# Small constants loaded at the end of the up-projections, half of a merge operand written in place, other operand loads cut into pieces

## The chip, the cores and the metric

The kernel runs on the 8 cores of one Trainium2 chip, in two dies of four cores (0 to 3 and 4 to 7). Each core computes one element of a batch of 8, with the same program and no traffic between cores. The metric is the device time of the slowest core, in microseconds (us).

Some executions fall into a slower state.

There is a smaller disturbance too: a few cores have some 160 us at a granted clock of 0.81, and such runs may still count as fast. (Core 0 of the kernel before has 0.81 in its trace's clock record from 75.0 to 236.2 us, with 6.8 us at 0.50 in between, which is 0.80 on average.)

- The **undisturbed cores** of a kernel: of all cores of all its runs, those whose mean clock lies within 0.0055 of the 90th percentile of that kernel's cores. I give the mean of their spans with its standard error.
- The **gain by stage**. The two kernels give TensorE the same instructions in the same order, and both profiles hold all 14317 weight loads. So the time of load number k in one profile, minus its time in the other, is what has been gained up to there, core by core.

## The reference, cut to what matters

```python
h = rms_norm(x, norm[l])
proj = h @ w_in[l]
# A: mLSTM: a short causal convolution (conv_w, conv_b) on q and k, gate biases, head norm (mh_norm)
qk = silu(causal_depthwise_conv(m_qk, conv_w[l], conv_b[l]))
ig = m_i + b_igate[l];  lf = log_sigmoid(m_f + b_fgate[l])
hm = rms_norm(mlstm_chunkwise(mq, mk, mv, ig, lf), mh_norm[l]) * sigmoid(m_o) * silu(m_z)
# B: latent attention
ha = causal_block_attention(qa, ka, v_a) * silu(a_z)
# C: cross attention into 256 memory tokens
hc = memory_attention(c_q, mkv[:, :, 0], mkv[:, :, 1]) * silu(c_z)
# gated merge and output projection
merged = g_m * (hm @ w_br_m[l]) + g_a * (ha @ w_br_a[l]) + g_c * (hc @ w_br_c[l])
x = x + merged @ w_out[l]
return rms_norm(x, final_norm)
```

With 2048 tokens and a width of 2048, `hm`, `ha` and `hc` are 2048 x 1024 each. They reach the merge through DRAM, as HMT, HAT and HCT, and are loaded half by half (1024 tokens, 2 MB).

## The kernel before

The program is written out in full by Python. Two generators are interleaved: a "dense" one (all projections, the merge, the output) and a "side" one (latent attention, then mLSTM, then cross attention). Each `yield` is a point where the other may put its instructions. `fw.op` and `fw.dma` derive the waits from what an instruction reads and writes; a DMA is issued by SyncE ("sp"), ScalarE ("act") or GpSimd ("pool"). A block's weights are 2 MB, loaded by GpSimd in four pieces when the block two before it is done:

```python
def w_done(name):
    wst["free"].append(wloaded.pop(name).slot)
    w_load()                 # 2 MB for the block after next starts here
```

The small constants are loaded at the head of the block that uses them, just after such a `w_done`:

```python
def qk_block(h):
    if h == 0:
        P["cw"] = mem.alloc("cw", [128, 16, 4], F32)
        P["cb"] = mem.alloc("cb", [128, 16], F32)
        fw.dma("sp", P["cw"][:], convw_d, writes=[P["cw"].r])
        fw.dma("sp", P["cb"][:], convb_d, writes=[P["cb"].r])
        # ...
                    act(y[:], bk[:, 0:512], AF.Identity, [r_bk, cw.r, cb.r], [y.r],
                        scale=cw[:, j, 3:4], bias=cb[:, j:j + 1])

def v_block(jv):
    if jv == 0:
        P["bif"] = mem.alloc("bif", [128, 8], F32)
        fw.dma("sp", P["bif"][:], bif_d, writes=[P["bif"].r])
    # ...

def oz_block(h):
    gmh = mem.alloc("gmh", [128, 256], F32)
    fw.dma("sp", gmh[:], gmh_d[:, h * 256:(h + 1) * 256], writes=[gmh.r])
    # ...
```

Cross attention: `loads` fetches queries of 256 KB (CQT), three buffers deep. `turn` transposes 128 tokens of the result and stores them through a ring of two buffers:

```python
def turn(t):
    # ... 8 transposes into btb
    o = hos.next()                       # a ring of 2
    copy("act", o[:], btb, [r_bt], [o.r])
    fw.dma("sp", HCT_d[t // 8, :, t % 8, :], o[:].rearrange("p a b -> p (a b)"), reads=[o.r], ...)
# ... per step of the loop:
    while turns:
        t = turns.pop(0)
        turn(t)
        if t == 7:
            marks.add("HC0")
        yield 0.6
```

The merge loads its operands while cross attention still runs:

```python
def hload(th, b):
    nm, src = (("HMT", HMT_d), ("HAT", HAT_d), ("HCT", HCT_d))[b]
    dims = "p a b c -> p (a b c)" if b != 1 else "p a b -> p (a b)"
    fw.dma("act", hb[b][:].rearrange(dims), src[th].rearrange("p a b -> p (a b)"), ...)   # 2 MB

def hm_ready():
    if "HM1" in marks and not hb:
        # ... allocate hb[0], hb[1], hb[2]
        hload(0, 0)
        hload(0, 1)
# ...
for u in range(LA):                      # LA = 4
    hm_ready()
    if u == LA - 2:
        yield ("need", "HM1")
        hm_ready()
        yield ("need", "HC0")
        hload(0, 2)
    yield from gate_unit(u, sring)       # 32 matmuls, a yield after every 8
```

The softmax here doesn't subtract the row's maximum and nothing guards it: scores larger than these inputs give would overflow.

## Time and profile before

| | before |
|---|---|
| time, median of 4 runs | 2923.26 us (2916.87 to 3257.57) |
| fast runs | 2920.87, 2925.64, 2916.87 us |
| profiled execution, slowest core | 2931.1 us (core 0) |
| TensorE busy on core 0 | 2753.6 us, 94% |
| five waits that the change aims at, core 0 | 10.66 + 9.88 + 4.99 + 16.29 + 3.11 = 44.9 us |

TensorE is the bottleneck (94% of the span busy, and 86% of the chain that ended last), so time can only be won where it idles or runs at a lowered clock. The last line is the DMA queue of ScalarE, with packets, MB and share of 16 engines' time; it carries the operand loads.

Die 0 had a stretch at 0.80 from 75 to 236 us and die 1 had not, as the windows of cores 0 and 4 show. (Columns: start and end in us, length, busy time and instructions of PE, PEld, DVE, ACT and POOL, the granted clock, the DMA share and GB/s.) First core 0:

```profile
75.00:236.00 161.00, 152.87 (x769) 73.82 (x783) 87.03 (x133) 66.17 (x165) 4.24 (x8) 0.80 0.36 98
```

and core 4:

```profile
75.00:236.00 161.00, 141.85 (x835) 69.91 (x832) 101.99 (x162) 67.50 (x168) 4.96 (x9) 0.99 0.38 107
```

In the same 161 us core 0 got through fewer weight loads (783 against 832) although it was busy for longer.

The timeline of TensorE on core 0 at the five waits. Each line is start, duration, engine, line, what it writes from what it reads; in brackets stands the idle time before it and what ended that:

```profile
453.06 0.37 PE L288 MATMUL bk<-Pa_68_3197,vx_52_2581 128*128 128x256 bf16 x1 [10.66 <-ACT Pa_68_3197 L292]
...
621.16 1.88 PE L288 MATMUL bk<-w_11_53,hT_8_50 128*128 128x258 bf16 x8 [9.88 <-DVE GIF_49 L301]
...
789.75 0.26 PE L288 MATMUL bk<-Pa_69_3198,vxb_63_3192 128*128 128x128 bf16 x1 [4.99 <-ACT Pa_69_3198 L292]
...
1685.84 1.01 PE L288 MATMUL bk<-cq_141_17856,kmT_3170 128*128 128x512 bf16 x2 [16.29 <-ACT ho_157_17946 L296]
...
1716.53 1.93 PE L288 MATMUL bk<-cq_142_17857,kmT_3170 128*128 128x512 bf16 x4 [3.11 <-ACT ho_157_17946 L296]
```

A releaser is often only the last link. The chain of waits around the first gap (start, duration, what) shows the rest:

```profile
436.79 14.92 DMA cb_3869<-convb
...
451.80 0.07 ACT y_89_3877 L292
...
452.63 0.29 ACT Pa_68_3197 L292
453.06 1.23 PE bk L288 x3
```

An 8 KB constant took 14.9 us to land. ScalarE stood still until then, and the exponentials that TensorE wanted (`Pa`) were queued behind. ScalarE's own waits (total us, times, longest) name the same constant, and for the fourth and fifth gap the store out of the buffer that `turn` reuses:

```profile
ACT ho_157_17946 L296 <- DMA HCT<-ho_157_17946: 26.4, 3, 17.5
...
ACT y_89_3877 L292 <- DMA cb_3869<-convb: 13.0, 1, 13.0
```

After each of these five waits TensorE ran at half its clock for a while. The trace's clock record of core 0 has 0.50 from 445.8 to 456.0, 616.4 to 626.7, 787.1 to 797.3, 1674.6 to 1691.6 and 1715.5 to 1722.3 us, that is until 2.9 to 7.6 us after the ends of the waits. Windows on core 0, the last one from deep in the merge:

```profile
453.00:456.00 3.00, 2.94 (x8) 1.20 (x9) 2.61 (x6) 1.91 (x5) 0.00 (x0) 0.50 0.00 0
...
1686.00:1692.00 6.00, 5.61 (x17) 1.92 (x16) 0.00 (x0) 2.68 (x5) 0.00 (x0) 0.53 0.52 132
1720.00:2720.00 1000.00, 993.83 (x4564) 454.36 (x4654) 138.91 (x216) 115.98 (x192) 258.82 (x314) 1.00 0.52 89
```

The clock is 0.50 and 0.53 in the two stretches after waits. In the last window TensorE is 99.4% busy at full clock: nothing can be won there.

### The profile page before, as it was taken

The page shows a single profiled execution, that of the slowest core. Times are in us where ns is not written, and L with a number is a line of the kernel's source. Part 1 is how long each engine was busy: PE and PEld are TensorE (multiplying, and loading weights), DVE is VectorE, ACT ScalarE, POOL GpSimd, SP SyncE. Part 2 cuts the span into 40 slices and gives each one's busy share as a digit, 9 for nine tenths or more (in the row PEclk, how much of TensorE's full clock was granted, in tenths as well). Part 3 has the DMA queues.
Part 4 walks back from the last instruction along what each step waited for, and adds up shares of the span by engine and source line. Part 5 has one row for each costly group of instructions (what it writes and reads, how often), then busy time and mean ns, then how long its engine had stood idle before and what let it go on. Part 6 is the DMA issues. An engine that isn't in the chain of part 4 may idle for free.

```text
span 2931.1 us, 42038 instructions; the slowest of 8 cores (2898.1 to 2931.1 us)
## 1 busy us (share of the span) xinstructions
PE 2753.6 (94%) x14042; PEld 1373.2 (47%) x14317; DVE 1104.5 (38%) x2091; ACT 813.5 (28%) x1672; POOL 498.9 (17%) x605
## 2 busy tenths in 40 slices
PE   4998998989999999999889799999999999999998
PEld 2443444566455754444444344444444444444443
DVE  3546537435657447545553331111111111111333
ACT  4523124323435335335444221111111111110111
POOL 0000300000010010124332012222222222222000
PEclk9789999999999999999999999999999999999999
DMA  7603642643443432444543654444455544446562
GB/s 195 188 15 120 179 114 56 136 96 66 108 108 78 109 93 60 97 132 129 138 123 112 176 140 76 78 74 76 79 117 121 104 76 76 77 78 107 189 213 86
DMA packets 143523, 322.16 MB, mean 110 GB/s; under 512 B 14800, under 2 KB 73104, under 8 KB 135120
## 3 DMA queue, kind: packets, MB, share of 16 engines
q0 software_dynamic: 42192, 134.79, 27.8%
q1 hardware_dynamic: 100256, 172.08, 18.6%
q10 hardware_dynamic: 864, 12.58, 1.1%
q8 instruction: 119, 1.95, 0.3%
q14 instruction: 92, 0.75, 0.1%
HBM read 380.38 MB, written 73.79 MB: 155 GB/s over the span
## 4 chain that ended last, share of the span: by engine, by line
PE 86%; DMA 5%; DVE 3%; issue 3%; ACT 2%; SPq 0%; DVEq 0%; POOL 0%; ACTq 0%; POOLq 0%
PE bk L288 85%; DMA xt_14_61<-x 1%; DMA HCT<-ho_158_17947 1%; DMA xt_13_60<-mem 1%; DMA cb_3869<-convb 1%; DMA bif_5641<-bif 0%; DMA xt_13_60<-x 0%; DMA mv_111_13609<-MV 0%; DMA gmh_7714<-g_mh 0%; PE bk L490 0%; DMA QNT<-ob_39_1819 0%; DVE Cf_13628 L308 0%; DMA KRT<-ob_38_1818 0%; DMA HCT<-ho_157_17946 0%; PE bk L516 0%
## 5 line engine op out<-in xcount | busy, mean ns | idle before, releaser
L288 PE MATMUL bk<-w_11_53,hT_8_50 128*128 128x512 bf16 (+1 forms) x1135 | 218.0, 344 | 15.7 <-DVE GIF_49 L301 11.7
L288 PE MATMUL bk<-w_11_53,hT_9_51 128*128 128x512 bf16 (+1 forms) x1132 | 218.5, 341 | 5.7 <-ACT hr_134_13632 L296 2.2
L288 PE MATMUL bk<-hT_8_50,w_10_52 128*128 128x512 bf16 x780 | 184.7, 379 | 5.3 <-ACT hr_134_13632 L296 2.2
L288 PE MATMUL bk<-hT_9_51,w_10_52 128*128 128x512 bf16 x778 | 184.8, 381 | 1.2
L288 PEld LDWEIGHTS bk<-w_11_53,hT_8_50 128*128 128x128 bf16 x1152 | 114.8, 101 | 102.2 <-issue 38.4
L288 PEld LDWEIGHTS bk<-w_11_53,hT_9_51 128*128 128x128 bf16 x1152 | 113.6, 100 | 87.6 <-issue 27.0
L288 PEld LDWEIGHTS bk<-hT_8_50,w_10_52 128*128 128x128 bf16 x800 | 77.3, 98 | 88.5 <-issue 4.9
L288 PEld LDWEIGHTS bk<-hT_9_51,w_10_52 128*128 128x128 bf16 x800 | 78.3, 98 | 84.9 <-issue 1.6
L288 PE MATMUL bk<-hT_8_50,wg_137_17736 128*128 128x512 bf16 x496 | 114.5, 383 | 0.8
L288 PE MATMUL bk<-hT_8_50,wg_138_17737 128*128 128x512 bf16 x498 | 114.4, 383 | 0.7
L308 DVE SCALAR_TENSOR_TENSOR tm_178_19271<-sh_183_19393,bk 128x512 f32<-128x512 f32 x31 | 21.3, 687 | 248.7 <-PE bk L288 248.7
L308 DVE SCALAR_TENSOR_TENSOR tm_178_19271<-sh_185_19395,bk 128x512 f32<-128x512 f32 x31 | 21.3, 687 | 247.5 <-PE bk L288 247.5
L288 PE MATMUL bk<-hT_8_50,wg_139_17738 128*128 128x512 bf16 x497 | 112.7, 379 | 0.8
L288 PE MATMUL bk<-hT_9_51,wg_138_17737 128*128 128x512 bf16 x499 | 112.4, 379 | 0.7
L288 PE MATMUL bk<-hT_9_51,wg_139_17738 128*128 128x512 bf16 x499 | 112.4, 379 | 0.7
L288 PE MATMUL bk<-hT_9_51,wg_137_17736 128*128 128x512 bf16 x496 | 111.8, 379 | 0.8
L292 ACT ACTIVATE sh_183_19393<-bk 128x512 f32<-128x512 f32 x46 | 27.5, 597 | 297.6 <-PE bk L288 297.6
L292 ACT ACTIVATE sh_185_19395<-bk 128x512 f32<-128x512 f32 x46 | 27.5, 597 | 290.2 <-PE bk L288 290.2
L288 PE MATMUL bk<-w_10_52,hT_8_50 128*128 128x512 bf16 x374 | 94.2, 398 | 10.0 <-ACT hT_8_50 L296 9.0
L288 PE MATMUL bk<-w_10_52,hT_9_51 128*128 128x512 bf16 x375 | 94.8, 403 | 0.7
L288 PEld LDWEIGHTS bk<-hT_8_50,wg_138_17737 128*128 128x128 bf16 x512 | 50.5, 99 | 61.5 <-issue 2.2
L288 PEld LDWEIGHTS bk<-hT_8_50,wg_137_17736 128*128 128x128 bf16 x512 | 50.4, 99 | 60.4 <-issue 2.2
(520 smaller groups left out, 4790.4 us busy)
## 6 DMA issues: line engine op xcount, KB each, us to landing
wg_137_17736<-wGB POOLq DMA_DIRECT2D x32, 512.0 KB, 5.1
wg_138_17737<-wGB POOLq DMA_DIRECT2D x32, 512.0 KB, 5.3
wg_139_17738<-wGB POOLq DMA_DIRECT2D x32, 512.0 KB, 5.1
w_10_52<-wA POOLq DMA_DIRECT2D x27, 516.0 KB, 10.7
w_11_53<-wA POOLq DMA_DIRECT2D x21, 516.0 KB, 11.9
xt_12_59<-x SPq DMA_DIRECT2D x6, 1024.0 KB
wb_171_18603<-wGB POOLq DMA_DIRECT2D x24, 256.0 KB, 4.5
wb_172_18604<-wGB POOLq DMA_DIRECT2D x24, 256.0 KB, 4.4
```

The costliest lines, as they stand in the source:

```text
L288: fw.op("pe", lambda e: e.matmul(bk[o] if not isinstance(o, bass.AP) else o, lhsT=lhsT, rhs=rhs, start=start, stop=stop), reads=reads, wri ...
L292: fw.op("act", lambda e: e.activation(out=out, in_=in_, func=func, **kw), reads=reads, writes=writes, accs=accs)
L308: fw.op("dve", lambda e: e.scalar_tensor_tensor(out=out, in0=in0, scalar=sc, in1=in1, op0=op0, op1=op1), reads=reads, writes=writes, accs= ...
```

## The change

The intent: issue the constants' loads long before they are needed, and no longer just after the 2 MB of weights that delayed them; take `turn`'s first eight tiles and one 2 MB load off the memory traffic; and load the two other operands in pieces, spread out, so that small urgent loads get through.

```diff
@@ end of the up-projections (about 350 us)
+            # cw, cb, bif and gmh[0] allocated and loaded here
+            fw.dma("sp", cw[:], convw_d, writes=[cw.r])
+            fw.dma("sp", cb[:], convb_d, writes=[cb.r])
+            fw.dma("sp", bif[:], bif_d, writes=[bif.r])
+            gmh_load(0)
@@ qk_block, v_block, oz_block: their own loads removed; gmh in two buffers, loaded ahead
-            gmh = mem.alloc("gmh", [128, 256], F32)
-            fw.dma("sp", gmh[:], gmh_d[:, h * 256:(h + 1) * 256], writes=[gmh.r])
+            gmh = P["gmh"][h % 2]
@@ mlstm_gen: only makes room for the constants
-            Cf = T("Cf", [128, 4, 2, 260], F32, n=4)        # also Cbs, hrs; PTs placed elsewhere
+            Cf = T("Cf", [128, 4, 2, 258], F32, n=4)
@@ c_gen
+            hb2 = P["hb2"] = mem.alloc("hb2", [128, 8, 8, 128], BF16)
@@ turn
+                if t < 8:
+                    copy("act", hb2[:, t, :, :], btb, [r_bt], [], accs=[hb2.r])
+                    return
@@ hload
-                fw.dma("act", hb[b][:].rearrange(dims), src[th].rearrange("p a b -> p (a b)"), ...)
+                for j in range(4):
+                    c = slice(j * 2048, (j + 1) * 2048)
+                    hq.append(lambda c=c, j=j: fw.dma("act", o[:, c], i[:, c], ...))
@@ d_gen (hm_ready and the HC0 mark removed)
+            yield ("need", "HM1")
+            hb = [mem.alloc("hb0", ...), mem.alloc("hb1", ...), P["hb2"]]
+            hload(0, 0)
+            hload(0, 1)
             for u in range(LA):
-                yield from gate_unit(u, sring)
+                for i, v in enumerate(gate_unit(u, sring)):
+                    if i % 2 == 0:
+                        hq.pop(0)()              # one 512 KB piece per 16 matmuls
+                    yield v
```

More of the change, by code (lines that the diff above doesn't have):

```diff
@@ L725, in p1_gen, with gmh_load @@
             P["e32"] = Ring(tiles("e32_", 2, [128, 512], F32))
+            cw = P["cw"] = mem.alloc("cw", [128, 16, 4], F32)
+            cb = P["cb"] = mem.alloc("cb", [128, 16], F32)
+            bif = P["bif"] = mem.alloc("bif", [128, 8], F32)
+            P["gmh"] = tiles("gmh", 1, [128, 256], F32)
+            fw.dma("sp", cw[:], convw_d, writes=[cw.r])
+            fw.dma("sp", cb[:], convb_d, writes=[cb.r])
+            fw.dma("sp", bif[:], bif_d, writes=[bif.r])
+            gmh_load(0)
             DB.items = banks[0:2]
             marks.add("MLA")
+        def gmh_load(h):
+            fw.dma("sp", P["gmh"][h % 2][:], gmh_d[:, h * 256:(h + 1) * 256], writes=[P["gmh"][h % 2].r])
         def silu2_evac(bk, r_bk, dst_d, dkey):
@@ L768, in qk_block @@
             if h == 0:
-                P["cw"] = mem.alloc("cw", [128, 16, 4], F32)
-                P["cb"] = mem.alloc("cb", [128, 16], F32)
-                fw.dma("sp", P["cw"][:], convw_d, writes=[P["cw"].r])
-                fw.dma("sp", P["cb"][:], convb_d, writes=[P["cb"].r])
                 P["pre"] = Ring(tiles("pre", 3, [128, 516], F32))
                 P["y"] = Ring(tiles("y", 3, [128, 512], F32))
+                P["gmh"] += tiles("gmg", 1, [128, 256], F32)
+                gmh_load(1)
             cw, cb = P["cw"], P["cb"]
@@ L813, in v_block @@
         def v_block(jv):
-            if jv == 0:
-                P["bif"] = mem.alloc("bif", [128, 8], F32)
-                fw.dma("sp", P["bif"][:], bif_d, writes=[P["bif"].r])
             bif = P["bif"]
@@ L856, in oz_block @@
             w_done("oz%d" % h)
-            mem.release(gmh)
+            if h < 2:
+                gmh_load(h + 2)
+            if h == 3:
+                mem.release(*P["gmh"])
         def cq_block(blk):
@@ L1068, in mlstm_gen @@
             DTs = tiles("DT", 2, [128, 4, 128], F32, top=True)
-            PTs = tiles("PT", 2, [128, 4, 128], BF16, top=True)
             qes = tiles("qe", 3, [128, 4, 2, 128], BF16, top=True)
             kws = tiles("kw", 2, [128, 4, 256], BF16, top=True)
-            Cf = T("Cf", [128, 4, 2, 260], F32, n=4)
-            Cbs = tiles("Cb", 2, [128, 4, 2, 260], BF16, n=4, top=True)
-            hrs = tiles("hr", 2, [128, 4, 260], F32, top=True)
+            Cf = T("Cf", [128, 4, 2, 258], F32, n=4)
+            Cbs = tiles("Cb", 2, [128, 4, 2, 258], BF16, n=4, top=True)
+            hrs = tiles("hr", 2, [128, 4, 258], F32, top=True)
             stm = Ring(tiles("stm", 2, [128, 16], F32, top=True))
+            PTs = tiles("PT", 2, [128, 4, 128], BF16)
             def loads(cp):
@@ L1292, in c_gen @@
                 while turns:
-                    t = turns.pop(0)
-                    turn(t)
-                    if t == 7:
-                        marks.add("HC0")
+                    turn(turns.pop(0))
                     yield 0.6
@@ L1355, in hload @@
                 nm, src = (("HMT", HMT_d), ("HAT", HAT_d), ("HCT", HCT_d))[b]
-                dims = "p a b c -> p (a b c)" if b != 1 else "p a b -> p (a b)"
-                fw.dma("act", hb[b][:].rearrange(dims), src[th].rearrange("p a b -> p (a b)"), reads=[dr(nm, th)], writes=[hb[b].r])
+                o = hb[b][:].rearrange("p a b c -> p (a b c)" if b != 1 else "p a b -> p (a b)")
+                i = src[th].rearrange("p a b -> p (a b)")
+                for j in range(4):
+                    c = slice(j * 2048, (j + 1) * 2048)
+                    hq.append(lambda c=c, j=j: fw.dma("act", o[:, c], i[:, c], reads=[dr(nm, th)], writes=[hb[b].r] if j == 0 else [], accs=[hb[b].r] if j else []))
+            hq = []
             def gate_unit(u, ring):
@@ L1374, in d_gen @@
             sring = Ring(sgs)
-            hb = []
-            def hm_ready():
-                if "HM1" in marks and not hb:
-                    hb.extend(mem.alloc("hb%d" % b, [[128, 4, 8, 256], [128, 8, 1024], [128, 8, 8, 128]][b], BF16) for b in range(3))
-                    hload(0, 0)
-                    hload(0, 1)
             wb = [mem.alloc("wb%d" % i, [128, 8, 128], BF16) for i in range(4)]
@@ L1384, in d_gen @@
                 bload()
+            yield ("need", "HM1")
+            hb = [mem.alloc("hb0", [128, 4, 8, 256], BF16), mem.alloc("hb1", [128, 8, 1024], BF16), P["hb2"]]
+            hload(0, 0)
+            hload(0, 1)
             for u in range(LA):
-                hm_ready()
-                if u == LA - 2:
-                    yield ("need", "HM1")
-                    hm_ready()
-                    yield ("need", "HC0")
-                    hload(0, 2)
-                yield from gate_unit(u, sring)
+                for i, v in enumerate(gate_unit(u, sring)):
+                    if i % 2 == 0:
+                        hq.pop(0)()
+                    yield v
             yield ("need", "HC1")
@@ L1442, in d_gen @@
                     hload(1, b)
+                    while hq:
+                        hq.pop(0)()
                 if th == 1 and c == 15 and b < 2:
```

## The prediction

> **What bounds the kernel.** TensorE: 2753.6 of 2931.1 us busy (94%, page), 86% of the chain of waits. From 1720 to 2720 us it is 99.4% busy at full clock (windows view); only idle gaps can be gained: 139 us in gaps over 0.7 us on core 0 (timeline).
>
> **What the change removes.** Five gaps, on core 0:
> 1. 10.7 us at 442: the first convolution evacuation waits for a constant of 8 KB, landed 14.9 us after issue, behind a 2 MB weight block (chain of waits).
> 2. 9.9 us at 611: the gate bias, 4 KB, 13.6 us.
> 3. 5.0 us at 785: the head-norm gain, 12.9 us. Other cores show 0 to 2.3 here.
> 4. 16.3 us at 1669: ScalarE waits 17.5 us for the HCT write out of the buffer it reuses. In flight: two 2 MB operand loads (landing 13.1 and 20.5 us) and weights. A 256 KB query load takes 24 us in the same stretch.
> 5. 3.1 us at 1713: the same wait beside the third operand load.
>
> Sum 45 us. Each gap also costs afterwards: [...]granted clock is 0.50 at 453 to 456, 0.53 at 621 to 627, 0.50 at 790 to 797, 0.53 at 1686 to 1692, 0.50 at 1717 to 1722. Half of these stretches is lost: about 14 us, an estimate from those windows. Together 59 us on core 0; core 2 (2928.2 us) 53, core 1 44, cores 5 and 6 about 47.
>
> **What it adds and moves.** TensorE's instruction order is unchanged. Eight ScalarE copies of about 1.0 us write to the merge operand instead of a buffer; eight stores of 256 KB and one 2 MB reload go away. The two remaining early loads become eight 512 KB pieces, one per 16 matmuls or so, each 0.35 to 0.7 us of ScalarE's queue, which has slack there. Four small loads move to about 358 us.
>
> **What stays.** At the head of the value block about 1.8 us (the second such block shows 1.81 us at 940); about 1 us in the other two heads. At 1669 the query load must still land beside 1 MB of weights and the first pieces: 2 to 3 us, an estimate. The last eight turns still go through memory: 1 to 2 us. Residue about 7 us. Other gaps are untouched.
>
> **Sum.** Core 0: 2931 - 59 + 7 = 2879; core 2: 2928 - 53 + 7 = 2882; the slowest core decides: about 46 us less. Fast runs before average 2923, so 2878 us, 1.6% faster. Range 2862 to 2897. Chances: faster by over 2% 0.17, within 2% 0.81, slower 0.02.
>
> **Checks.** Right if the waits on the constants vanish, the gap at 1669 falls under 4 us, the clock stays 1.0 at 445 to 456 and 616 to 627, and after 1720 all is as before, shifted. Wrong if a new wait on the query load takes over at 1669, if the pieces land late for the first merge unit, or if other waits (score tiles, 2-bank evacuation) fill the freed gaps.
>
> **What would make it wrong.** [...] (die 0 shows 0.81 from 75 to 236 us). Residues may be nearly zero and the gap at 1633 may shrink too; then it passes 2%.

45 us of waits and 14 us of clock go and 7 us come, so 2931 - 59 + 7 = 2879 us on core 0. Of the 7 us only the 1.8 us is read from a trace (the second value block); the rest is estimate.

## More of the kernel before

The head of the profile's page of the kernel before: the span, the busy time of each engine, and the clock that TensorE was granted, in tenths for each of 40 equal slices. (The page holds 14042 of the 14317 matmul records.)

```profile
span 2931.1 us, 42038 instructions; the slowest of 8 cores (2898.1 to 2931.1 us)
...
PE 2753.6 (94%) x14042; PEld 1373.2 (47%) x14317; DVE 1104.5 (38%) x2091; ACT 813.5 (28%) x1672; POOL 498.9 (17%) x605
...
PEclk9789999999999999999999999999999999999999
...
q10 hardware_dynamic: 864, 12.58, 1.1%
```

The view of all cores:

```profile
core 0: 2931.1 us, clock 0.970
...
core 7: 2898.1 us, clock 0.982
die 0 (median of its cores): 2921.3 us, clock 0.971
die 1 (median of its cores): 2905.5 us, clock 0.980
```

The dies are 15.8 us apart.

## The result, and the profile after

| | before | after |
|---|---|---|
| median of 4 runs | 2923.26 us | 2879.78 us (2876.12 to 3307.57) |
| fast runs | 2920.87, 2925.64, 2916.87 us | 2882.39, 2876.12, 2877.18 us |
| ratio of fast runs | | 0.9854, 95% interval 0.9824 to 0.9884 |
| die 1 in the profile, median of its cores | 2905.5 us | 2864.0 us |

A ratio here is the mean time of one kernel's fast runs over that of the other's from the same rounds, so it is not quite the ratio of the medians. The change made the kernel 1.5% faster, which is within 2%. The result is correct.

The head of the page after:

```profile
span 2881.3 us, 42326 instructions; the slowest of 8 cores (2853.5 to 2881.3 us)
...
PE 2739.6 (95%) x14317; PEld 1363.0 (47%) x14317; DVE 1105.2 (38%) x2091; ACT 813.3 (28%) x1672; POOL 498.9 (17%) x605
...
PEclk8999999999999999999999999999999999999999
...
q10 hardware_dynamic: 2880, 10.49, 1.1%
```

ScalarE's queue moves 2 MB less, in more and smaller packets. (Of the 288 instructions more, 275 are matmul records that the profile of before had missed.) The view of all cores:

```profile
core 1: 2881.3 us, clock 0.985
...
die 0 (median of its cores): 2867.2 us, clock 0.987
die 1 (median of its cores): 2864.0 us, clock 0.987
```

The dies are equal now; the stretch at 0.81 is missing in this execution (from 75 to 236 us the clock averages 0.98 to 0.99 on all 8 cores, where before it was 0.80 to 0.81 on the cores of die 0). So die 0's gain of 54.1 us in these two profiles is not all the change's; die 1's 41.5 us, or 1.4%, is the cleaner figure.

The three waits on constants are gone. It is the lead that removed them: the constants still go out beside the 2 MB of another block (on core 1 at 351.8 to 354.6 us, the weights at 351.3 to 352.9 us), but cb is now issued some 70 us before its first use, where before it was 2 us before the moment at which it was wanted. Where the first one stood, core 1 is now busy throughout at full clock, in the same columns as the windows before:

```profile
415.00:440.00 25.00, 25.00 (x129) 12.28 (x128) 16.23 (x28) 11.25 (x24) 2.11 (x4) 1.00 0.69 127
```

TensorE's waits on core 1 (total us, times, longest) show what remains at the end of cross attention. The wait on the query load (`cq`) has come in place of the 16 us on the store:

```profile
PE bk L288 <- DMA cq_140_17857<-CQT: 5.0, 1, 5.0
...
PE bk L288 <- ACT ho_156_17947 L296: 3.5, 1, 3.5
```

Here is the gain by stage, made from both profiles with the method above. The stages are times in the kernel before:

```
us gained       0-420   420-560   560-660   660-820   820-1600   1600-1750   rest   total
                      conv head  value head head norm           cross att. end
core 0           19.6       8.9      12.7       8.8       -4.4        20.0    0.2    65.9
core 1           14.4      11.3      12.6       1.8      -13.1         6.7   -0.8    32.9
core 2           16.9      10.4      10.5       2.6       -2.5        19.9    1.4    59.1
core 3           14.0      11.8      10.3       0.1        1.6        15.6    0.0    53.5
core 4            1.5      12.1       8.0      -0.0        1.3        16.7    0.0    39.7
core 5            2.1      13.3      10.1       1.3       -1.5        16.8    0.7    42.7
core 6            2.4       9.7      10.2       2.7        0.1        17.9    0.1    43.2
core 7            5.8       8.1       9.6       0.3        1.7        18.7    0.2    44.5
```

Die 0 gained 14 to 20 us before 420 us (die 1: 1.5 to 5.8), where the stretch at 0.81 had been. The change touches nothing that is executed there but the issue of the constants at about 350 us. From there on the dies look alike: on the mean of 8 cores 23.4 us come from the three heads of blocks, 16.5 us from the end of cross attention, and nothing after 1750 us. Core 1 gained only 6.7 us at the end of cross attention and lost 13.1 us between 820 and 1600 us, which made it the slowest. Most variants below also have cores that lose 4 to 13 us in that stretch, core 1 above all (the rerun of the changed kernel has four that lose 10 to 13).

One more thing came out of this alignment. At one wait that both kernels have, on the same instruction and of the same length, what followed was different. First the kernel before, core 0: the timeline, then a window after the wait:

```profile
521.47 1.02 PE L288 MATMUL bk<-twof_48,den_70_3199 128*128 128x1 f32 x8 [2.00 <-DVE rta_77_3206 L298]
```

and the window:

```profile
521.50:523.00 1.50, 1.50 (x12) 1.14 (x12) 1.33 (x3) 0.72 (x2) 0.00 (x0) 1.00 0.94 163
```

Now the kernel after, core 0, likewise:

```profile
489.67 1.50 PE L288 MATMUL bk<-twof_48,den_74_3208 128*128 128x1 f32 x8 [2.00 <-DVE rta_81_3215 L298]
```

and the window:

```profile
491.00:493.00 2.00, 2.00 (x6) 0.74 (x7) 1.20 (x3) 0.00 (x0) 0.00 (x0) 0.50 1.00 185
```

In the clock record of the kernel after, the clock fell to 0.50 at 490.04 us, 0.37 us after the end of that wait, and stayed there until 496.87 us, so the 1.50 us of the next matmuls (1.02 us before) already contain some of the loss. The same 2.00 us cost core 0 a spell at half clock in one kernel and none in the other (1.00 from 519.5 to 528 us); in the stages core 0 loses 3.3 us between 480 and 560 us. Other cores win or lose some 1.7 us there. Why the outcome differs is not shown. From these 3.3 and 1.7 us I estimate that one profile of one core can't show differences of less than 2 to 3 us.

### The profile page after: what moved, and what is told of

It is laid out like the page before. It is cut to its first block, busy times and chain, and to the rows that moved or that the text cites. A ratio compares the mean times of both kernels' runs of the same rounds, so it can differ in the third digit from the quotient of the medians.

```text
span 2881.3 us, 42326 instructions; the slowest of 8 cores (2853.5 to 2881.3 us)
## 1 busy us (share of the span) xinstructions
PE 2739.6 (95%) x14317; PEld 1363.0 (47%) x14317; DVE 1105.2 (38%) x2091; ACT 813.3 (28%) x1672; POOL 498.9 (17%) x605
## 3 DMA queue, kind: packets, MB, share of 16 engines
q10 hardware_dynamic: 2880, 10.49, 1.1%
## 4 chain that ended last, share of the span: by engine, by line
PE 87%; DMA 5%; DVE 3%; ACT 3%; issue 2%; SPq 0%; DVEq 0%; ACTq 0%; POOL 0%; POOLq 0%
PE bk L288 86%; DMA mv_109_13609<-MV 1%; DMA xt_14_61<-x 1%; DMA xt_14_61<-mem 1%; DMA cq_140_17857<-CQT 1%; DVE xb_15_62 L308 0%; DMA xt_13_60<-x 0%; DMA QNT<-ob_39_1819 0%; PE bk L490 0%; DMA HCT<-ho_157_17948 0%; SPq L132 0%; DVE Cf_13626 L308 0%; DMA KRT<-ob_38_1818 0%; DMA mb_113_13613<-BH 0%; ACT hm_102_13602 L296 0%
## 5 line engine op out<-in xcount | busy, mean ns | idle before, releaser
L288 PE MATMUL bk<-w_11_53,hT_9_51 128*128 128x512 bf16 (+1 forms) x1152 | 212.3, 333 | 6.6 <-ACT hr_130_13630 L296 2.2
L288 PE MATMUL bk<-w_11_53,hT_8_50 128*128 128x512 bf16 (+1 forms) x1152 | 208.5, 333 | 4.3 <-DVE GIF_49 L301 1.8
```

The source lines that it names most:

```text
L288: fw.op("pe", lambda e: e.matmul(bk[o] if not isinstance(o, bass.AP) else o, lhsT=lhsT, rhs=rhs, start=start, stop=stop), reads=reads, wri ...
```

## The experiments

All compare with the kernel before on the same chip. Three calls went to three chips, whose undisturbed cores of the kernel before took 2902.3 ± 1.2, 2904.0 ± 1.2 and 2908.3 ± 1.4 us. The gains by stage compare each one's single profile with the one profile of before that is read above, which came from another chip; 2 or 3 us in them mean nothing. All results were correct.

```
                  ratio of fast runs       undisturbed cores,   gain by stage, mean of 8 cores, us
                  (95% interval)           us against before    420-820 (constants)  1600-1750 (cross att.)
chip of call 1
e1_const          0.9991 (0.9906-1.0077)   -17.0 +- 2.3               23.4                -1.7
e2_direct         1.0056 (0.9949-1.0163)    -3.2 +- 2.3                1.3                 7.6
e3_pieces         1.0027 (0.9960-1.0095)    -3.2 +- 1.8                2.2                 3.6
e5_just_ahead     1.0001 (0.9917-1.0084)   -13.5 +- 1.8               23.8                -1.8
chip of call 2
after_again       0.9875 (0.9852-0.9899)   -34.9 +- 1.7               22.2                15.2
e6_no_const       0.9933 (0.9913-0.9952)   -15.2 +- 2.0                1.9                17.3
e4_more           0.9809 (0.9786-0.9833)   -47.9 +- 1.6               22.8                19.1
e7_at_once        one run, 2883.37 us      -37.3 +- 3.3               23.2                13.8
chip of call 3
e9_by_partition   0.9909 (0.9869-0.9948)   -25.2 +- 2.1               23.0                -0.4
e8_whole_spaced   0.9880 (0.9852-0.9907)   -31.6 +- 2.1               23.4                 9.8
e10_fine          0.9781 (0.9763-0.9798)   -55.9 +- 1.7               24.5                18.3
```

On the chip of call 1 the ratios could not tell the parts apart: lowered clocks moved the slowest core by more than the parts did. In the profiled runs the mean clock was 0.972 and 0.975 on cores 2 and 3 in `e1_const`, 0.963 on cores 2 and 3 and 0.972 and 0.973 on cores 6 and 7 in `e2_direct` (where the four had 0.79 to 0.81 from 75 to 236 us), and 0.975 and 0.973 on cores 4 and 5 in `e5_just_ahead`, against 0.980 to 0.984 on the other cores. For the parts I rely on the other two columns. The choice of undisturbed cores goes by the clock, so it favours cores with fewer spells at half clock, in every kernel alike. It also depends a little on how the percentile is taken: interpolated between two cores, it gives -14.1 for `e6_no_const` and -35.3 for `e7_at_once`, and the other rows stay within 0.1.

### The parts one at a time

My theory: the constants and the end of cross attention are two separate gains, and at the end of cross attention the operand loads hold up both the store of `turn` and the query load. The rival: one part alone carries it, for example the direct copy.

`e1_const` has the constants loaded early (and the smaller strides that make room), the rest as before:

```diff
 # from the changed kernel, undone:
-                if t < 8:
-                    copy("act", hb2[:, t, :, :], btb, [r_bt], [], accs=[hb2.r])
-                    return
-                for j in range(4): ...                     # pieces
+                fw.dma("act", hb[b][:].rearrange(dims), src[th]...)
```

> Only the early constants (and the smaller strides that make room for them). My account: the gaps at the first convolution (7 to 11 us), the value block (6 to 10) and, on one core, the head norm (5) go, with about 2 us of half-clock work after each; the median core of die 1 gets 17 to 20 us shorter, ratio 0.993 to 0.995; the gap at the end of cross attention (10 to 17 us) stays. Rival: TensorE only waits elsewhere (score tiles, two-bank evacuation); then under 8 us, ratio above 0.997, and new gaps within 30 us of the old places.

Measured: 2933.91 us median of 6 runs (before on this chip 2953.51 of 11), ratio 0.9991, which can't be told from 1 (the expected 0.993 to 0.995 did not show, as explained above). Undisturbed cores gained 17.0 us. By stage, the constants gave 23.4 us, as much as in the full change. The end of cross attention kept its wait, as the timeline of core 4 shows:

```profile
1641.61 1.01 PE L288 MATMUL bk<-cq,kmT 128*128 128x512 bf16 x2 [16.82 <-ACT ho L296]
```

`e2_direct` has only the direct copy; both remaining operand loads stay whole:

```diff
+                if t < 8:
+                    copy("act", hb2[:, t, :, :], btb, [r_bt], [], accs=[hb2.r])
+                    return
-                    hb.extend(mem.alloc("hb%d" % b, ...) for b in range(3))
+                    hb.extend([mem.alloc("hb0", ...), mem.alloc("hb1", ...), P["hb2"]])
-                    yield ("need", "HC0")
-                    hload(0, 2)
```

> Only the first half written straight into the merge operand; the two other operands still come as 2 MB loads at once. Theory A (too much in flight): ScalarE no longer waits for a store, but the 256 KB query load still takes over 15 us beside the 4 MB, so TensorE waits 8 to 15 us in the same place, now for that load; gain under 10 us, ratio above 0.9965. Theory B (the buffer's reuse was the cause): the gap falls under 4 us and the gain is 17 to 22 us, ratio 0.992 to 0.994.

Measured: 2946.38 us median of 6 runs, undisturbed cores 3.2 us better. The wait on the store is gone, and another has taken its place. Core 4:

```profile
1645.34 1.86 PE L288 MATMUL bk<-cq,kmT 128*128 128x512 bf16 x4 [14.88 <-DMA cq<-CQT]
```

This is the wait on the query load, which had stood hidden beside the wait on the store. On all 8 cores it was 13.7 to 15.4 us. So theory A holds.

`e3_pieces` has only the pieces: three loads of four pieces, two of them paced from the first gate units:

```diff
+                for j in range(4):
+                    c = slice(j * 2048, (j + 1) * 2048)
+                    (hq2 if (th, b) == (0, 2) else hq).append(lambda c=c, j=j: fw.dma("act", o[:, c], i[:, c], ...))
+                for i, v in enumerate(gate_unit(u, sring)):
+                    q = hq if i % 2 == 0 else hq2
+                    if q:
+                        q.pop(0)()
+                    yield v
```

> Only the pieces: all three first operands in 512 KB pieces, the cross attention half still through memory. Theory A: store and query load land within 8 us, the gap of 10 to 17 us shrinks to 2 to 6 us, gain 10 to 18 us, ratio 0.994 to 0.9965. Theory B: the wait for the store remains 8 us or more and the gain is under 8 us.

Measured: 2932.91 us median of 8 runs, undisturbed cores 3.2 us better. Neither theory had it right: the waits shrank as A said, but the gain was as small as B said. The one long wait broke into several short ones: 2.4 to 4 us on the store, then 1.1 to 4.4 us on the query load, and later one of 3.7 to 8.1 us on one of the two. Core 1:

```profile
1648.46 1.01 PE L288 MATMUL bk<-cq,kmT 128*128 128x512 bf16 x2 [3.80 <-ACT ho L296]
```

`e6_no_const` has the direct copy and the pieces together, without the early constants:

```diff
 # from the changed kernel, undone:
-            fw.dma("sp", cw[:], convw_d, writes=[cw.r])    # at the end of the up-projections; also cb, bif, gmh
+                fw.dma("sp", P["cw"][:], convw_d, writes=[P["cw"].r])     # back in qk_block, and so on
```

> Direct half and pieces together, constants late as before. If the two parts remove two waits that stand side by side, so that either alone leaves the other, they gain together 15 to 20 us on undisturbed cores, though 3 each alone; the gap at the end of cross attention is under 5 us and the gaps at the first convolution and the value block are as before (7 to 10 us each). If the parts simply add, 6 us.

Measured: 2907.18 us median, ratio 0.9933, undisturbed cores 15.2 us better. The waits on the constants are kept as intended, and those at the end of cross attention are short. Core 4:

```profile
433.86 0.37 PE L288 MATMUL bk<-Pa,vx 128*128 128x256 bf16 x1 [9.10 <-ACT Pa L292]
...
1641.84 1.51 PE L288 MATMUL bk<-cq,kmT 128*128 128x512 bf16 x4 [4.09 <-DMA cq<-CQT]
```

What follows: the rival falls. The direct copy alone (3.2 us) and the pieces alone (3.2 us) sum to 6.4 us, and together they give 15.2 us. By stage it is 7.6 and 3.6 against 17.3 us. Two waits stood side by side: with the direct copy alone the one on the query load took the place of the one on the store, and with the pieces alone both stayed, shorter, and a third came after them. The constants are a separate gain: their 17.0 us and the 15.2 us of the rest sum to 32.2 us, and the whole change gives 34.9 ± 1.7 us on the chip of call 2.

### The changed kernel again

`after_again` is the changed kernel, word for word.

> The changed kernel once more, beside its own halves. On cores whose clock record shows no stretch at 0.81, it should be 33 to 38 us under the kernel before (2902 against 2867 so far, from two chips). That is more than the 17 of the constants alone plus 3 and 3 of the other two parts alone.

Measured: four fast runs from 2887.36 to 2897.56 us and four slow ones (median of all 2945.3), ratio 0.9875. The waits at the end of cross attention on core 1 were 2.67 and 3.75 us, both on the query load. The longest on the other cores were 2.0 to 5.2 us, except on core 2, where the query load still cost 10.7 us. The total repeats on another chip, and the change does not cure this wait on every core in every execution.

### Why a constant of 8 KB took 15 us

Two causes fit the trace of before: the load was issued too late for any load, or it was issued together with 2 MB of weights and landed with them. In all 8 cores the constant was used within 2 us of the landing of the last weight piece, for instance on core 0 (us):

```
                      weights landed    constant used
conv head                 451.5             451.8
value head                622.2             620.8    (third of four pieces: 619.8)
head norm                 786.8             788.0
```

`e5_just_ahead` issues each constant only some 15 us earlier than before (the expectation says 10): 7 to 10 us before the block of weights and not just after it, and 16 to 17 us before its use:

```diff
 def gate_block(name, ...):          # the block before
+                    if (ci, tb) == (3, 1):
+                        if name == "az0":
+                            # alloc and load cw, cb
+                        else:
+                            # alloc and load bif
 def qk_block(h):
+                    if (h, ci, tb) == (1, 3, 1):
+                        # alloc and load the first gmh
```

> The kernel before, with the constants issued only three quarters of the last quarter before their block, some 10 us earlier than before and ahead of the 2 MB weight load that their block's start sets off, not 80 to 430 us earlier. If their lateness is the weight load in front of them, they land within 4 us and the gain is that of the early constants within 4 us. If a load of this kind needs longer because of its many small packets, 5 us or more of each gap stay.

Measured: the three waits were gone on all 8 cores. The stage of the constants gained 23.8 us, against 23.4 us with a lead of 70 us and more. That alone does not settle it, since a load that takes 15 us for reasons of its own would also be in time with a lead of 16 to 17 us. The landings do: on the 8 cores the 4 KB of bif landed 1.7 to 2.7 us after issue (on core 0 of the kernel before they were used 13.7 us after it) and the 32 KB of cw 2.0 to 2.1 us after. The second gmh, which this version still issues just after its weights, took 11.6 to 14.1 us. From the DMA view of core 0, in the windows 566 to 567 and 978 to 979 us (KB, and us to landing):

```profile
bif<-bif SPq DMA_DIRECT2D x1, 4.0 KB, 2.4
...
gmh<-g_mh SPq DMA_DIRECT2D x1, 128.0 KB, 12.2
```

So the weights in front are what made the loads late. Either cure suffices: going ahead of the weights, as here, or a long lead beside other weights, as in the changed kernel. (The undisturbed cores gained 13.5 us against 17.0 in `e1_const`, a difference of 3.5 ± 2.4 us; the stages put no part of it on the constants.) The loads were issued by different engines, the constants by SyncE (queue q1) and the weights by GpSimd (q0), and still the same 4 KB took 1.7 to 2.7 us ahead of the weights and 13.6 us behind them.

### What in the pieces helps: their number, their shape or their spacing

With whole loads TensorE waits 14 to 15 us for the query load, and in the profile after the change 2.8 to 5.0 us (2.0 to 10.7 us in the rerun). Three properties changed at once: the transfer is smaller (512 KB), its packets are smaller (a column slice has 4 KB contiguous per partition in place of 16 KB), and the pieces are spaced out. The packets can be counted. Before, six loads of 128 partitions and 16 more packets each make 6 x 144 = 864; after, twenty pieces make 20 x 144 = 2880, which are the numbers in the pages above.

`e7_at_once` keeps the pieces by column and issues all eight at once:

```diff
-    NS = {"sp": 16, "pool": 8, "act": 6}
+    NS = {"sp": 16, "pool": 8, "act": 8}
+            while hq:
+                hq.pop(0)()
             for u in range(LA):
-                for i, v in enumerate(gate_unit(u, sring)):
-                    if i % 2 == 0:
-                        hq.pop(0)()
-                    yield v
+                yield from gate_unit(u, sring)
```

> The changed kernel with all eight 512 KB pieces issued at once before the first gate unit. If pacing is what helps, the gap of 13 to 15 us on the query load is back, as with the two 2 MB loads. If it is the smaller size of the transfers, the gap stays under 6 us.

`e9_by_partition` is `e7_at_once` cut the other way: pieces of 32 partitions and full rows. Size, number and moment of issue are equal; the packets differ, 16 KB against 4 KB (and the partitions that one piece goes to, 32 against 128):

```diff
-                    c = slice(j * 2048, (j + 1) * 2048)
-                    hq.append(lambda c=c, j=j: fw.dma("act", o[:, c], i[:, c], ...))
+                    c = slice(j * 32, (j + 1) * 32)
+                    hq.append(lambda c=c, j=j: fw.dma("act", o[c], i[c], ...))
```

> As the run with all eight pieces at once, and pieces of the same 512 KB, but cut by partition (32 rows of 16 KB) and not by column (128 rows of 4 KB): the same bytes at the same moment, in packets of 16 KB instead of 4 KB. If the queues take turns by packet, the query load, in packets of 1 KB, waits four times as long per turn: the gap before the scores is 12 to 16 us as with two whole loads, not 4 to 10. If the number or size of the transfers counts, the gap stays at 4 to 10 us.

`e8_whole_spaced` spaces two whole 2 MB loads by two gate units:

```diff
-                for j in range(4):
-                    c = slice(j * 2048, (j + 1) * 2048)
+                for j in range(1 if th == 0 else 4):
+                    c = slice(0, 8192) if th == 0 else slice(j * 2048, (j + 1) * 2048)
-                    if i % 2 == 0:
+                    if (u, i) in ((0, 0), (2, 0)):
```

> The changed kernel with its two first operands as whole 2 MB loads again (16 KB packets), but spaced: one before the first gate unit, one before the third. If the packet size is what counts, gaps on the query load of 5 to 12 us appear at the first of them, less than 15 because only half the bytes are in flight, and undisturbed cores lose 5 to 12 us against the changed kernel. If spacing alone suffices, gaps stay under 5 us and the time is that of the changed kernel within 3 us.

Measured: the longest wait on the query load was 4.4 to 10.3 us in `e7_at_once` (one run, 2883.37 us), 22.1 to 25.1 us in `e9_by_partition` (2894.13 us, ratio 0.9909), and 4.7 to 10.0 us in `e8_whole_spaced` (2886.12 us, ratio 0.988), which also kept waits of 2.8 to 7.1 us on the store. The first lies between the two cases that were expected, the second is longer than expected, and the third is as expected if the packet size counts. One line of each timeline, `e7_at_once` on core 1 first:

```profile
1641.19 1.86 PE L288 MATMUL bk<-cq,kmT 128*128 128x512 bf16 x4 [9.48 <-DMA cq<-CQT]
```

then `e9_by_partition`, core 1:

```profile
1635.66 1.87 PE L288 MATMUL bk<-cq,kmT 128*128 128x512 bf16 x4 [22.14 <-DMA cq<-CQT]
```

and `e8_whole_spaced`, core 0:

```profile
1628.53 1.87 PE L288 MATMUL bk<-cq,kmT 128*128 128x512 bf16 x4 [10.02 <-DMA cq<-CQT]
```

Cutting alone does nothing, then: by partition it is even worse than two whole loads at once (`e2_direct`, 13.7 to 15.4 us). The DMA view suggests why. It covers 15 us on core 1 while the operand loads were under way, with packets, MB and share of 16 engines; q10 carries the operands, q1 the query load and SyncE's other transfers. With whole loads (`e2_direct`):

```profile
q10 hardware_dynamic: 235, 3.59, 66.4%
...
q1 hardware_dynamic: 259, 0.49, 11.4%
```

by column (`e7_at_once`):

```profile
q10 hardware_dynamic: 486, 1.80, 36.4%
q1 hardware_dynamic: 722, 0.94, 23.9%
```

by partition (`e9_by_partition`):

```profile
q10 hardware_dynamic: 182, 2.13, 60.6%
...
q1 hardware_dynamic: 363, 0.55, 14.5%
```

Per packet of q10, q1 sent 1.1, 1.5 and 2.0 packets (1.1, 1.5 and 2.5 without the 4-byte packets that both queues also hold), while the data packets of q10 were 16, 4 and 16 KB. Per byte of q10, q1 sent 0.14, 0.52 and 0.26 bytes. So in these three windows what q1 got through went more with the packets of q10 than with its bytes. Beside 16 KB packets q1, where the query load has packets of 1 KB, got about half the bytes through in the same time (0.49 and 0.55 against 0.94 MB). In the traces of before and after, a packet of q10 took 0.61 us with 16 KB and 0.16 us with 4 KB (medians, core 0). All this would fit queues that take turns by packet, as `e9_by_partition` supposed; how the turns are made is not shown. The order of landing fits too. In `e2_direct` and `e9_by_partition` the operands are 256 packets of 16 KB, and on all 8 cores TensorE got its queries only 1.5 to 2.1 us and 0.4 to 0.6 us after the last operand had landed. In `e7_at_once` they are 1024 packets of 4 KB, and it got them 7.9 to 12.7 us before the last operand landed.

Beside small packets spacing shows no gain clear of the noise: `e7_at_once` took 2866.7 ± 3.1 us on undisturbed cores and the changed kernel 2869.1 ± 1.2 on the same chip; by stage the changed kernel is 1.4 to 2.7 us ahead. Spacing of whole loads (`e8_whole_spaced`) seems worth less than small packets: by stage 9.8 us against 13.8, each from a single profile. Left open: why the 16 KB packets of `e9_by_partition` took 1.17 us each and those of whole loads 0.61 us (medians). They go to 32 partitions in place of 128, but no run separates that, so part of the 22.1 to 25.1 us may come from the partitions and not from the packet size.

### Two versions that go further

The timeline after the change still showed waits of about 5 us near 244 and near 312 us (4.95 and 5.13 us on core 1, with a clock of 0.50 until 248.6 and 316.9 us): one large sine and cosine on ScalarE, and a ring of three output buffers. `e4_more` adds to the changed kernel:

```diff
-            act(sinT[:], sinT[:], AF.Sin, ...)
-            act(cosT[:], cosT[:], AF.Sin, ...)
+            for qq in range(4):                       # in quarters, with yields between
+                qc = slice(qq * QW, (qq + 1) * QW)
+                act(sinT[:, qc], sinT[:, qc], AF.Sin, ...)
+                yield
+                act(cosT[:, qc], cosT[:, qc], AF.Sin, ...)
+                yield
-            ob = Ring(tiles("ob", 3, [128, S], BF16))
+            ob = Ring(tiles("ob", 5, [128, S], BF16))
-            for _ in range(4):
-                bload()
+                bload()                               # one per gate unit
```

> The changed kernel with three more waits taken away: sine and cosine of the angles in quarters (gap of 5.0 us at 244), five output buffers for three in the up-projections (gap of 3 to 5 us at 312), and the first four branch weights, 1 MB that lands just when the last query loads are due, loaded one per gate unit. Theory: about 9 us of idle and some 5 us of half-clock work go, and the gap of 3 to 5 us on the query load falls to 1 to 2; gain over the changed kernel 10 to 16 us. Rival: the wait at 312 is for the stores themselves, which queue behind weight loads, and comes back elsewhere; then under 8 us.

Measured: 2874.18 us median of 8 runs, ratio 0.9809; undisturbed cores 47.9 us better than before, so 13.0 us better than the changed kernel on the same chip. Both waits are gone on core 1: between 230 and 320 us no wait above 1.5 us is left.

`e10_fine` adds to that pieces of 256 KB (2 KB packets), one per 8 matmuls:

```diff
-    NS = {"sp": 16, "pool": 8, "act": 6}
+    NS = {"sp": 16, "pool": 8, "act": 12}
-                for j in range(4):
-                    c = slice(j * 2048, (j + 1) * 2048)
+                for j in range(8):
+                    c = slice(j * 1024, (j + 1) * 1024)
-                    if i % 2 == 0:
-                        hq.pop(0)()
+                    hq.pop(0)()
```

> The best version so far (sine in quarters, five output buffers, branch weights one per gate unit) with the early operand loads in pieces of 256 KB, 2 KB packets, one before each eight matmuls. If smaller packets still help, the waits of 3 to 4 us for the store and 2.5 us for the query load shrink to 1 to 2 and the time falls by 2 to 4 us; otherwise the same within 2 us.

Measured: 2861.65 us median of 6 runs (2858.11 the lowest), ratio 0.9781 with an interval of 0.9763 to 0.9798: faster than the kernel before by over 2%, and the best of all. What the finer pieces add is not settled. By stage the end of cross attention gains 18.3 us, against 19.1 in `e4_more`, and the undisturbed cores of the two (2852.4 and 2856.1 us) are from different chips. Core 1 still waits for the query load:

```profile
1641.87 1.60 PE L288 MATMUL bk<-cq,kmT 128*128 128x512 bf16 x4 [3.04 <-DMA cq<-CQT]
```

## Why the prediction was right, point by point

- **The total: right.** It said 2878 us; the median was 2879.78. It said 1.6%; the ratio of fast runs says 1.5%.
- **What bounds the kernel: right.** Nothing changed after 1750 us (-0.8 to 1.4 us by stage), and all gains came from idle time and the clock.
- **The constants: right.** The three waits vanished on every core, and `e1_const` shows that they are a gain of their own.
- **"At the head of the value block about 1.8 us", and 1 us at the other heads: wrong.** No wait of 0.7 us or more was left at the three first heads. The second value block kept its 1.81 us, which means that the analogy with it failed.
- **"About 14 us" for the clock: too large.** On core 0 the stages of the five waits gained 8.9 + 12.7 + 8.8 + 20.0 = 50.4 us. The five waits themselves were 44.9 us, and the two waits on the query load at the end of cross attention grew by 1.3 us in sum (2.13 and 1.41 us before, 2.77 and 2.08 us after). So some 7 us are left for the clock. The old half-clock spells did vanish, but new ones came: 3.3 us lost after the unchanged wait of 2.00 us at 489 us, and the clock was 0.72 to 0.78 in the 6 us after each of the two waits on the query load.
- **"Residue about 7 us": too large**, since on core 0 only those 1.3 us came. The two wrong terms nearly cancel, which is luck: 45 + 14 - 7 = 52 us predicted on core 0, 50.4 us measured in these stages.
- **The wait at 1669 us: mostly right.** It was to fall under 4 us. It did on six cores. On core 1 it was 5.0 us and on core 5 4.5 us, both on the query load: the new wait that the prediction named as a danger. On core 1 it left this stage with 6.7 us of gain, where 15.6 to 20.0 were had on the others. In the rerun two cores were over 4 us there, one of them at 10.7 us.
- **"About 46 us less": somewhat too large.** The ratio of fast runs says 42.6 us (1.46% of the 2921.1 us that the fast runs of before average). On clean cores it is 41.5 us for die 1 in the two profiles, and 34.9 ± 1.7 us or 1.2% for the undisturbed cores on the chip of call 2; how much of that difference is the chip and how much the choice of cores is open. The stretch at 0.81 on die 0, which the prediction named, did no harm to it, as the gain was summed from waits and not from the spans of cores. But that the slowest core of the profile, 2881 us, stands so near the 2882 us of the sum is luck in part: the sum has the stretch in it, and in the profile after it was missing, while core 1 lost 13.1 us between 820 and 1600 us that the prediction does not have.
- **What it did not see:** the two parts at the end of cross attention each give 3.2 us alone and 15.2 us together. It priced the wait on the store by its own 16.3 us, and noted the query load of 24 us beside it, but did not say that either part would be nearly worthless without the other. It also did not say which property of the pieces helps: their size, their packets or their spacing.

## What to carry to other kernels

A small load that TensorE will wait for should be issued just before a large one starts, not just after: here 4 KB landed 1.7 to 2.7 us after issue ahead of 2 MB of weights and 13.6 us after it behind them, and 16 to 17 us of lead ahead of the weights were as good as 70 us beside them. When a small load must run beside large ones on another queue, try to cut the large ones so that each contiguous row is short: pieces with rows of 4 KB cut the wait here (4.4 to 10.3 us, against 13.7 to 15.4 us beside whole loads), and pieces of fewer rows of the full 16 KB did not (22.1 to 25.1 us). Before crediting a wait to what ended it, look for a second one that stands beside it, as removing either alone may bring nearly nothing (here 3.2 us each, and 15.2 us together), and compare cores of equal clock: the stretch at 0.81 on die 0 alone stood beside a difference of 15.8 us between the dies in the profile before.
